# Rearranging the opening of a hybrid attention and RG-LRU block: a broadcast by DMA, scale matrices and casts on GpSimd, one extra product

## The chip, the cores and the metric

The kernel runs on one core of one Trainium2 chip. A core has five engines that run their own instruction streams and meet through semaphores: TensorE (PE, with its weight loads shown as PEld), VectorE (DVE), ScalarE (ACT), GpSimd (POOL) and SyncE (SP), which here only issues DMAs. The metric is the device time of one execution in microseconds.

## The reference, cut to what matters

One decoder layer with a final norm: x is 1024 x 1024 fp32 (sequence by model width), c is one row of 1024. Only the first lines matter for this change:

```python
mod = c @ w_ada[l] + b_ada[l]
shift, scale, gate = jnp.split(mod, 3, axis=-1)
h = rmsnorm(x, norm_g[l]) * (1.0 + scale[:, None, :]) + shift[:, None, :]
proj = h @ w_in[l]
q, k, v, g_attn, xr, g_rnn, m_attn, m_rnn = jnp.split(proj, SPLIT_POINTS, axis=-1)
```

Behind it come sliding-window attention with sinks and partial rotary embedding (angle = position times a frequency), a gated linear recurrence (RG-LRU) behind a short convolution, two projections, a merge by sigmoid gates, an output projection, the residual and a last RMSNorm.

## The kernel before

Every large product is made in three matmuls of half-precision-like parts: each operand is cast to a high part (fp32r) and the rest, and high x high, rest x high and high x rest are summed. The large input projection behind the opening goes over pairs of output columns with seven half-size products for eight, in an order that a small planner writes out; attention and the two projections follow. None of that is changed.

The change is in the opening (lines 184 to 489), which makes h, transposed, in eight row blocks of 128 of its 1024 columns (index `kc`), and multiplies the first four column chunks of `w_in` (`START`, chunks 0, 1, 34 and 35, called `c` 0 to 3 there) with it. Its engines run in exactly the order in which the code issues (`manual_schedule`, line 181), each engine its own instructions, so an instruction that waits holds up all that stands behind it on its engine. The steps:

- Loads. On SP: eight tiles of x (`xt`, 128 x 1024, 512 KB each), then `w_ss`, the transposed modulation weights (`load_ss(kc)`: two 512 KB tiles for a `kc`), and halves of the first weight chunks (`load_s`), in turns. On ACT's queue: c as two half rows, and `pk`, a 128 x 96 table of small parameters. On POOL's queue: positions (`posr`) and the rotary frequencies (`invf`).
- c on all partitions. Two fp32 products on PE (line 248) with a row of ones put c into PSUM for 128 partitions; DVE copies them to `c_bc` (lines 384 and 385).
- Norm and transposes, a loop over the eight tiles of x (lines 390 to 398). `square(i)` on ACT sums the squares; `mean(i)` on DVE; `root(i-1)` on ACT; `scaled(i-1)` on DVE takes the reciprocal and scales the tile, or, for the tiles in `DIAG` (0 and 2), makes a diagonal matrix `dg` instead (line 346), by which PE scales while it transposes; `flip(i-1)` on PE makes eight 128 x 128 transposes into PSUM (line 359, or line 361 as a matmul with `dg`). `out_of(j, p, engine)` copies transposed blocks to SBUF (`xT`), on ACT (line 367) or DVE (line 369); the table `late` says at which turn of the loop.
- Modulation. `modulate(kc)` on DVE (line 258): two products of `w_ss` tiles with `c_bc`, summed along the row. `scales_of(kc)` on ACT (lines 263 and 265) makes scale and shift of the 128 rows, with `bng` (line 381) as an offset. `hi_parts(kc)` on ACT (lines 375 and 378) makes the high part `hh` in two halves and the full value; `lo_parts(kc)` on DVE (line 421) the rest `hl`.
- Weights. `cast_s(c, i)` on ACT (line 100) makes the high part `wh` of a half chunk, `rest_s(c, i)` on DVE (line 106) the rest `wl`. `first(kc, terms, cs)` on PE (line 434) makes the products: "h" is wh x hh, "w" is wl x hh, "l" is wh x hl. The first of them, `first(0, "h", (2, 3, 0, 1))`, needs `hi_parts(0)` and the four casts; `first(1, "h")` needs `hi_parts(1)`; `first(0, "w")` needs the four rests.
- Rotary angles. `angles()` on POOL (lines 286 to 321): 36 small steps on 128 x 64 and 128 x 128 tiles, wanted by a sine on ACT in line 469. Before the change they are issued all at once, ahead of the loop, and nothing else of the opening is behind them on POOL.

The last of the opening's work on ACT, in order: four `out_of(2, p)`, casts of c 2 and 3, `out_of(3, 0)`, `scales_of(0)`, `hi_parts(0)`, cast of c 0, `out_of(3, 3)`, cast of c 1, `scales_of(1)`, `hi_parts(1)`.

Of the kernel before, what the change touches and what calls it, by code (L numbers as in the profile page):

```python
# [12 lines left out]
F32 = mybir.dt.float32  # L13
# [5 lines left out]
ALU = mybir.AluOpType  # L19
# [3 lines left out]
P = 128  # L23
S = 1024
D = 1024
KC = 8
HALF = 512
# [6 lines left out]
PK_C, PK_BSH, PK_BSC, PK_NG, PK_CW, PK_CB, PK_BA, PK_BX, PK_LAM = (  # L34
    0, 8, 16, 24, 32, 64, 72, 80, 88)
# [9 lines left out]

SL = [slice(0, HALF), slice(HALF, S)]
XT = 12
DIAG = 0, 2


@with_exitstack
def tile_hybrid_block(ctx, tc, x, pk, rows, posr, posi, invf, c_row, w_ss, w_gate, w_main, w_v,
                      w_g, w_ap, w_rp, w_out, out):
    nc = tc.nc
    V, A, G, T = nc.vector, nc.scalar, nc.gpsimd, nc.tensor

# [23 lines left out]
    pk_t = const.tile([P, PK_N], F32, name="pk_t")  # L80
    ident = const.tile([P, P], F32, name="ident")
# [16 lines left out]
    def cast(dst, src, scale=1.0):  # L98
        if scale == 1.0:
            A.copy(dst[0][:], src)  # L100
        else:
            A.activation(dst[0][:], src, AF.Copy, scale=scale)  # L102
# [81 lines left out]
    starts = [new_ps(), new_ps(), bk[2:], bk[:2]]  # L184
    N_ST = len(starts)
    START = (0, 1, 34, 35)
    with ExitStack() as st:
        sp = st.enter_context(tc.tile_pool(name="start", bufs=1, side="right"))
        c_row_t = [wp.tile([P, HALF], F32, tag="ws", name="c_row_t", bufs=3)[0:1, :]
                   for _ in range(2)]  # L190
        for i in range(2):
            dma(c_row_t[i], c_row[:, SL[i]], A)
        dma(pk_t[:], pk, A)
        posr_t = sp.tile([P, 64], I32, name="posr_t")
        dma(posr_t[:], posr, G)
        invf_t = sp.tile([P, 1], F32, name="invf_t")
# [3 lines left out]
        xt, wada = [], {}  # L200
        for i in range(8):
            t = sp.tile([P, D], F32, tag="xt", name="xt", bufs=XT)
            dma(t[:], x[i * P:(i + 1) * P, :])
            xt.append(t)

        def load_ss(kc):
            for a in (1, 0):
# [4 lines left out]
        sw = [[None, None] for _ in starts]  # L212
        raw = {}
# [1 line left out]
        def load_s(c, i):  # L215
            raw[c, i] = load_half(w_main[START[c]][:, SL[i]])

        def cast_s(c, i):
            sw[c][i] = slot()
            cast(sw[c][i], raw[c, i])  # L220

        def rest_s(c, i):
            rest(sw[c][i], raw[c, i])
# [13 lines left out]
            load_ss(kc)  # L237
        rv = [load_half(w_v[i // 2][:, SL[i % 2]]) for i in range(4)]

        one_row = sp.tile([1, P], F32, name="one_row")  # L240
        warm = sp.tile([P, 1], F32, name="warm")
        V.memset(warm[:], 1.0)
        V.memset(one_row[:], 1.0)
        A.activation(warm[:], warm[:], AF.Sqrt)
        c_bc = sp.tile([P, D], F32, name="c_bc")
        psc = starts[0]
        for hf in range(2):
            T.matmul(psc[hf], one_row[:], c_row_t[hf], start=True, stop=True)
# [22 lines left out]
        def rnd(name, src, unit, n=64):  # L271
            m = 1.5 * 2.0 ** 23 * unit
            t = tiny(name, n)
            G.tensor_scalar(out=t[:], in0=src, scalar1=m, scalar2=m, op0=ALU.add,
                            op1=ALU.subtract)
            return t

        def pair_of(name, a, b, op=ALU.subtract, n=64):
            t = tiny(name, n)
            G.tensor_tensor(out=t[:], in0=a, in1=b, op=op)  # L280
            return t
# [4 lines left out]
        def angles():  # L286
            posf, ang = tiny("posf"), tiny("ang")
            G.tensor_copy(posf[:], posr_t[:])
            G.tensor_scalar(out=ang[:], in0=posf[:], scalar1=invf_t[:, 0:1], scalar2=None,
                            op0=ALU.mult)  # L290
            units = (2.0 ** 20, 2.0 ** 9, 2.0 ** -3)
            cons = [_split_const(u) for u in units]
            sums, tmp = [tiny(n) for n in ("sa", "sb", "sc_")], tiny("tmp")
            left = ang
            for i, unit in enumerate(units):
                piece = rnd(f"t{i}", left[:], unit)
                left = pair_of(f"a{i}", left[:], piece[:])
                for which, t in enumerate(sums):
                    k = float(cons[i][which] / unit)
                    o = t if i == 0 else tmp  # L300
                    G.tensor_scalar(out=o[:], in0=piece[:], scalar1=k, scalar2=None,
                                    op0=ALU.mult)
                    if i:
                        G.tensor_tensor(out=t[:], in0=t[:], in1=tmp[:], op=ALU.add)
            sa, sb, sc_ = sums
            ra = rnd("ra", sa[:], 1.0)
            fa = pair_of("fa", sa[:], ra[:])
            tt = pair_of("tt", fa[:], sb[:], ALU.add)
            rt = rnd("rt", tt[:], 1.0)
            ft = pair_of("ft", tt[:], rt[:])  # L310
            G.tensor_scalar(out=tmp[:], in0=left[:], scalar1=1.0 / (2.0 * math.pi),
                            scalar2=None, op0=ALU.mult)
            G.tensor_tensor(out=sc_[:], in0=sc_[:], in1=tmp[:], op=ALU.add)
            G.tensor_tensor(out=trn[:, 1, :], in0=ft[:], in1=sc_[:], op=ALU.add)
            G.tensor_scalar(out=trn[:, 0, :], in0=trn[:, 1, :], scalar1=0.25, scalar2=None,
                            op0=ALU.add)
            r2 = rnd("r2", trf, 1.0, 128)
            G.tensor_tensor(out=trf, in0=trf, in1=r2[:], op=ALU.subtract)
            G.tensor_scalar(out=trf, in0=trf, scalar1=2.0 * math.pi, scalar2=3.1415925,
                            op0=ALU.mult, op1=ALU.min)  # L320
            G.tensor_scalar(out=trf, in0=trf, scalar1=-3.1415925, scalar2=None, op0=ALU.max)

        ss = tiny("ss", 8)
        rr = tiny("rr", 8)
# [13 lines left out]
        def scaled(i):  # L338
            r1 = rr[:, i:i + 1]
            V.reciprocal(r1, r1)  # L340
            if i not in DIAG:
                V.tensor_scalar(out=xt[i][:], in0=xt[i][:], scalar1=r1, scalar2=None,
                                op0=ALU.mult)
            else:
                dg[i] = sp.tile([P, P], F32, tag="dg", name="dg", bufs=2)
                V.tensor_scalar(out=dg[i][:], in0=ident[:], scalar1=r1, scalar2=None,
                                op0=ALU.mult)

        dg = {}
# [3 lines left out]
        def flip(i):  # L353
            for kc in range(KC):
                c0 = kc // 4 * 256 + i % 2 * P
                o = banks[i // 2 % 2][kc % 4][:, c0:c0 + P]
                x_ = xt[i][:, kc * P:(kc + 1) * P]
                if i not in DIAG:
                    T.transpose(o, x_, ident[:])
                else:  # L360
                    T.matmul(o, x_, dg[i][:], start=True, stop=True)

        def out_of(j, p, eng):
            src = banks[j % 2][p].rearrange("p (a t) -> p a t", a=2)
            dst = xall[p][:, :, j * 256:(j + 1) * 256]
            if eng is A:
                A.copy(dst, src)
            else:
                V.tensor_copy(dst, src)

        def hi_parts(kc):
# [41 lines left out]
        out_of(3, 3, A)  # L413
        cast_s(1, 0)
        modulate(1)
        csn = sp.tile([P, 3, 64], F32, name="csn")

# [1114 lines left out]
    late, high, loaded = [], [], {}  # L1532
# [285 lines left out]
```

## Time and profile before

| what | value |
|---|---|
| median of three runs | 941.1 us (939.51 to 945.45) |
| the profiled execution's own time | 942.38 us |
| its span, first to last instruction | 940.3 us |
| PE busy in the span | 916.8 us (98%) |
| DVE, ACT, POOL busy | 679.5, 543.2, 119.3 us |
| mean granted TensorE clock | 0.994 |
| DMA moved | 164.21 MB, mean 175 GB/s |

A row of the timeline gives the start in us from the start of the span, the length, the engine, the line, the operation, the tiles written and read (output first), the shapes, how many instructions are merged in the row, and in brackets how long the engine was idle before it and what ended that. A row of the stage view gives the stretch, its length, the busy time of PE, PEld, DVE, ACT and POOL in it, the granted clock, the DMA engines' busy share and GB/s. A row of the chain gives start, length and what. In a row of groups the figures behind the bar are total busy us and mean ns of one, then idle time before them. A row of DMA issues ends in the median us from issue to landing.

### The profile page before, as it was taken

The page shows a single profiled execution, that of the slowest core. Times are in us where ns is not written, and L with a number is a line of the kernel's source. Part 1 is how long each engine was busy: PE and PEld are TensorE (multiplying, and loading weights), DVE is VectorE, ACT ScalarE, POOL GpSimd, SP SyncE. Part 2 cuts the span into 40 slices and gives each one's busy share as a digit, 9 for nine tenths or more (in the row PEclk, how much of TensorE's full clock was granted, in tenths as well). Part 3 has the DMA queues.
Part 4 walks back from the last instruction along what each step waited for, and adds up shares of the span by engine and source line. Part 5 has one row for each costly group of instructions (what it writes and reads, how often), then busy time and mean ns, then how long its engine had stood idle before and what let it go on. Part 6 is the DMA issues. An engine that isn't in the chain of part 4 may idle for free.

```text
span 940.3 us, 12460 instructions
## 1 busy us (share of the span) xinstructions
PE 916.8 (98%) x4277; PEld 754.9 (80%) x4277; DVE 679.5 (72%) x1003; ACT 543.2 (58%) x1053; POOL 119.3 (13%) x218
## 2 busy tenths in 40 slices
PE   6899999999999999999999999999999999999997
PEld 5689877888888788888888887788888888888886
DVE  5998597777659955885786786798999737656522
ACT  6866545554567755966585874787887622212311
POOL 6320050000000000000000001354454300000000
PEclk9899999999999999999999999999999999999999
DMA  9815578471332532452334258897656186536311
GB/s 346 317 55 202 179 268 268 141 268 52 113 113 101 172 128 71 145 201 90 113 112 157 101 169 259 282 369 226 217 177 195 57 308 221 168 130 219 135 73 68
DMA packets 80919, 164.21 MB, mean 175 GB/s; under 512 B 12532, under 2 KB 28916, under 8 KB 80856
## 3 DMA queue, kind: packets, MB, share of 16 engines
q1 hardware_dynamic: 77732, 156.02, 48.6%
q0 software_dynamic: 2256, 6.03, 2.0%
q10 hardware_dynamic: 868, 1.36, 0.4%
q8 instruction: 34, 0.56, 0.3%
q14 instruction: 29, 0.24, 0.1%
HBM read 114.00 MB, written 49.78 MB: 174 GB/s over the span
## 4 chain that ended last, share of the span: by engine, by line
PE 72%; DVE 10%; DMA 10%; ACT 5%; issue 3%; SPq 0%; POOL 0%; ACTq 0%; DVEq 0%
PE bk L628 40%; PE rp L169 7%; PE pgate L937 5%; PE rp L1683 3%; PE pmain L1683 3%; DMA wo<-w_out 3%; PE pmain L434 2%; PE bk L434 2%; PE pv L1251 2%; PE s_ps L1178 2%; DMA smr<-smr_d 1%; DMA tt<-tr_d 1%; PE pt L1217 1%; DVE wl L106 1%; DMA r<-w_ap 1%
## 5 line engine op out<-in xcount | busy, mean ns | idle before, releaser
L628 PE MATMUL bk<-nh,wh 128*128 128x512 f32 x368 | 145.1, 394 | 0.0
L628 PE MATMUL bk<-nl,wh 128*128 128x512 f32 x368 | 144.4, 392 | 0.0
L628 PE MATMUL bk<-nh,wl 128*128 128x512 f32 x368 | 143.0, 389 | 0.0
L106 DVE TENSOR_TENSOR wl<-r,wh 128x512 fp32r<-128x512 f32 x109 | 79.2, 733 | 14.3 <-ACT wh L100 14.2
L100 ACT CAST wh<-r 128x512 fp32r<-128x512 f32 x109 | 67.0, 618 | 34.6 <-DMA r<-w_ap 11.8
L628 PEld LDWEIGHTS bk<-nl,wh 128*128 128x128 f32 x368 | 69.1, 188 | 15.9
L628 PEld LDWEIGHTS bk<-nh,wl 128*128 128x128 f32 x368 | 69.2, 188 | 15.5
L628 PEld LDWEIGHTS bk<-nh,wh 128*128 128x128 f32 x368 | 69.3, 188 | 14.6 <-ACT wh L102 0.9
L628 PE MATMUL bk<-hh,wh 128*128 128x512 f32 x184 | 72.4, 394 | 0.0
L628 PE MATMUL bk<-hl,wh 128*128 128x512 f32 x184 | 72.2, 392 | 0.0
L628 PE MATMUL bk<-hh,wl 128*128 128x512 f32 x184 | 71.5, 388 | 0.0
L106 DVE TENSOR_TENSOR wl<-ws,wh 128x512 fp32r<-128x512 f32 x76 | 51.5, 684 | 4.4 <-ACT wh L100 4.4
L1203 ACT ACTIVATE p<-p,small 128x129 f32<-128x129 f32 x128 | 50.1, 401 | 0.0
L100 ACT CAST wh<-ws 128x512 fp32r<-128x512 f32 x76 | 45.7, 615 | 3.2 <-DVE ws L650 1.5
L628 PEld LDWEIGHTS bk<-hl,wh 128*128 128x128 f32 x184 | 34.5, 188 | 8.0
L1178 PE MATMUL s_ps<-ks,qs 128*128 128x256 f32 (+1 forms) x256 | 38.6, 294 | 2.3 <-DMA qs<-q_d 2.2
L628 PEld LDWEIGHTS bk<-hh,wl 128*128 128x128 f32 x184 | 34.5, 188 | 7.7
L628 PEld LDWEIGHTS bk<-hh,wh 128*128 128x128 f32 x184 | 34.6, 188 | 6.9
L802 POOL MEMSET xr<- 128x3 f32 x8 | 0.8, 101 | 309.9 <-PE pgate L937 233.4
L628 PE MATMUL bk<-hha,wl 128*128 128x512 f32 x92 | 36.1, 392 | 2.1 <-DVE wl L106 1.5
L741 ACT ACTIVATE c<-bk 128x512 f32<-128x512 f32 x29 | 17.3, 597 | 34.3 <-PE bk L628 34.2
L1700 ACT ACTIVATE o<-xo 128x1024 f32<-128x1024 f32 (+2 forms) x10 | 8.9, 890 | 47.5 <-DVE xo L1699 47.5
(351 smaller groups left out, 2297.1 us busy)
## 6 DMA issues: line engine op xcount, KB each, us to landing
r<-w_main SPq DMA_DIRECT2D x100, 256.0 KB, 4.2
wada<-w_ss SPq DMA_DIRECT2D x16, 512.0 KB, 8.2
qs<-q_d SPq DMA_DIRECT2D x16, 512.0 KB, 5.4
ks<-k_d SPq DMA_DIRECT2D x24, 192.0 KB, 3.8
xt<-x SPq DMA_DIRECT2D x8, 512.0 KB, 8.0
sma_d<-c SPq DMA_DIRECT2D x16, 256.0 KB, 3.5
wg<-w_gate SPq DMA_DIRECT2D x8, 512.0 KB, 5.1
q_d<-rhi SPq DMA_DIRECT2D x16, 256.0 KB, 4.6
```

The source lines that it names most:

```text
L100: A.copy(dst[0][:], src)
L106: V.tensor_tensor(out=dst[1][:], in0=src, in1=f32(dst[0][:]), op=ALU.subtract)
L169: mm = T.matmul(ps[hf], ww, xx[kc][hf], start=(kc == 0 and ww is w_h and xx is xh), stop=(kc == KC - 1 and xx is xl))
L434: T.matmul(starts[c][hf], ww[:, c0:c0 + P], xh[kc][hf], start=(kc == 0 and t_ == "h"), stop=(kc == KC - 1 and t_ == "l"))
L628: W["pe"] = T.matmul(ps, ww[:, c], b[kc][xx_], start=(first and kc == 0 and i == 0), stop=(kc == 3 and i == 2), skip_group_check=not first)
L741: A.activation(t["t"], s(), AF.Tanh, scale=0.5)
L937: W["pe"] = T.matmul(ps[:, SL[hf]], ww[:, c0:c0 + P], xx_[:, SL[hf]], start=(ic == 0 and i == 0), stop=(ic == 1 and i == 2))
L1178: W["pe"] = T.matmul(o, qs[:, j, qc], ks[:, b, k0 + (0 if n else P):k0 + 256], start=(b == 0), stop=(b == 1))
L1203: A.activation(px[:, j, :], px[:, j, :], AF.Exp, bias=sm[:, 0, j:j + 1], accum_out=sm[:, 1, j:j + 1])
L1217: W["pe"] = T.transpose(pt[:, j, :], px[:, j, 0:P], ident[:])
L1251: W["pe"] = T.matmul(pv[:], b, m[:].rearrange("p j q -> p (j q)"), start=(i == 0), stop=(i == len(prods) - 1))
L1683: T.matmul(ps[:, sl], lhs[k][th][:, ts_], w[:, sl], start=(k == 0 and w is h_ and lhs is mh), stop=(k == KC - 1 and lhs is ml))
```

## The change

- c comes to all partitions by one DMA on SP (a row of DRAM read for 128 partitions, 512 KB written), behind the eight x tiles; the two half rows, the row of ones, the two products and the two copies are gone. `pk` is loaded on SP behind it instead of on ACT's queue.
- `DIAG` gets tile 4, so that tile is scaled by PE too; the diagonal matrices are made on POOL.
- `angles()` becomes a generator that yields behind each step. Three steps are issued ahead of the loop, four behind each `scaled(i-1)`, and the last five behind the casts.
- The copies `out_of` are dealt out anew between DVE and ACT; `bng` moves behind `modulate(0)` on DVE.
- The four first casts go to POOL, in one go behind the loop and ahead of the last angle steps.
- Behind the last transposes PE gets one fp32 product, the identity by half of x tile 6, into a bank that the next product overwrites.

```diff
-DIAG = 0, 2
+DIAG = 0, 2, 4
...
-        c_row_t = [wp.tile([P, HALF], F32, tag="ws", name="c_row_t", bufs=3)[0:1, :]
-                   for _ in range(2)]
-        for i in range(2):
-            dma(c_row_t[i], c_row[:, SL[i]], A)
-        dma(pk_t[:], pk, A)
...
+        c_bc = sp.tile([P, D], F32, name="c_bc")
+        dma(c_bc[:], c_row.to_broadcast([P, D]))
+        dma(pk_t[:], pk)
...
-        def cast_s(c, i):
+        def cast_s(c, i, eng=A):
             sw[c][i] = slot()
-            cast(sw[c][i], raw[c, i])
+            if eng is G:
+                G.tensor_copy(sw[c][i][0][:], raw[c, i])
+            else:
+                cast(sw[c][i], raw[c, i])
...
-        for hf in range(2):
-            T.matmul(psc[hf], one_row[:], c_row_t[hf], start=True, stop=True)
...
             G.tensor_copy(posf[:], posr_t[:])
+            yield 1
             G.tensor_scalar(out=ang[:], in0=posf[:], scalar1=invf_t[:, 0:1], scalar2=None,
                             op0=ALU.mult)
+            yield 1
...
-                V.tensor_scalar(out=dg[i][:], in0=ident[:], scalar1=r1, scalar2=None,
+                G.tensor_scalar(out=dg[i][:], in0=ident[:], scalar1=r1, scalar2=None,
                                 op0=ALU.mult)
...
-        angles()
-        late = {1: [lambda: V.scalar_tensor_tensor(
-                    out=bng[:], in0=pk_t[:, PK_BSC:PK_BSC + 8], scalar=1.0,
-                    in1=pk_t[:, PK_NG:PK_NG + 8], op0=ALU.add, op1=ALU.mult),
-                    lambda: V.tensor_copy(c_bc[:, SL[0]], psc[0])],
-                2: [lambda: V.tensor_copy(c_bc[:, SL[1]], psc[1])],
-                3: [lambda: out_of(0, 0, V), lambda: out_of(0, 1, V)],
-                4: [lambda: out_of(0, 2, V), lambda: out_of(0, 3, V)],
+        angle = angles()
+
+        def turn(n=100):
+            for _ in range(n):
+                if next(angle, 0) == 0:
+                    break
+
+        turn(3)
+        late = {3: [lambda: out_of(0, 0, V), lambda: out_of(0, 1, V)],
+                4: [lambda: out_of(0, 2, V), lambda: out_of(0, 3, A)],
                 5: [lambda: out_of(1, 0, V), lambda: out_of(1, 1, V)],
-                6: [lambda: out_of(1, 2, A), lambda: out_of(1, 3, A)]}
+                6: [lambda: out_of(1, 2, A), lambda: out_of(1, 3, V)]}
...
                 root(i - 1)
                 scaled(i - 1)
+                turn(4)
                 flip(i - 1)
...
         flip(7)
-        for c in (2, 3):
-            cast_s(c, 0)
+        for i in range(1):
+            T.matmul(bk[i], ident[:], xt[6][:, SL[i]], start=True, stop=True)
+        for c in (2, 3, 0, 1):
+            cast_s(c, 0, G)
+        turn()
         modulate(0)
-        out_of(3, 0, A)
+        V.scalar_tensor_tensor(out=bng[:], in0=pk_t[:, PK_BSC:PK_BSC + 8], scalar=1.0,
+                               in1=pk_t[:, PK_NG:PK_NG + 8], op0=ALU.add, op1=ALU.mult)
+        for p in range(3):
+            out_of(3, p, A)
         scales_of(0)
         hi_parts(0)
-        out_of(3, 1, V)
-        cast_s(0, 0)
-        out_of(3, 2, V)
-        out_of(3, 3, A)
-        cast_s(1, 0)
+        out_of(3, 3, V)
         modulate(1)
```

More of the change, by code (lines that the diff above doesn't have):

```diff
@@ L238, in tile_hybrid_block @@
         rv = [load_half(w_v[i // 2][:, SL[i % 2]]) for i in range(4)]
-        one_row = sp.tile([1, P], F32, name="one_row")
         warm = sp.tile([P, 1], F32, name="warm")
         V.memset(warm[:], 1.0)
-        V.memset(one_row[:], 1.0)
         A.activation(warm[:], warm[:], AF.Sqrt)
-        c_bc = sp.tile([P, D], F32, name="c_bc")
-        psc = starts[0]
-        for hf in range(2):
-            T.matmul(psc[hf], one_row[:], c_row_t[hf], start=True, stop=True)
         mods = sp.tile([P, 16], F32, name="mods")
@@ L296, in angles @@
                 piece = rnd(f"t{i}", left[:], unit)
+                yield 1
                 left = pair_of(f"a{i}", left[:], piece[:])
+                yield 1
                 for which, t in enumerate(sums):
@@ L302, in angles @@
                                     op0=ALU.mult)
+                    yield 1
                     if i:
                         G.tensor_tensor(out=t[:], in0=t[:], in1=tmp[:], op=ALU.add)
+                        yield 1
             sa, sb, sc_ = sums
             ra = rnd("ra", sa[:], 1.0)
+            yield 1
             fa = pair_of("fa", sa[:], ra[:])
+            yield 1
             tt = pair_of("tt", fa[:], sb[:], ALU.add)
+            yield 1
             rt = rnd("rt", tt[:], 1.0)
+            yield 1
             ft = pair_of("ft", tt[:], rt[:])
+            yield 1
             G.tensor_scalar(out=tmp[:], in0=left[:], scalar1=1.0 / (2.0 * math.pi),
                             scalar2=None, op0=ALU.mult)
+            yield 1
             G.tensor_tensor(out=sc_[:], in0=sc_[:], in1=tmp[:], op=ALU.add)
+            yield 1
             G.tensor_tensor(out=trn[:, 1, :], in0=ft[:], in1=sc_[:], op=ALU.add)
+            yield 1
             G.tensor_scalar(out=trn[:, 0, :], in0=trn[:, 1, :], scalar1=0.25, scalar2=None,
                             op0=ALU.add)
+            yield 1
             r2 = rnd("r2", trf, 1.0, 128)
+            yield 1
             G.tensor_tensor(out=trf, in0=trf, in1=r2[:], op=ALU.subtract)
+            yield 1
             G.tensor_scalar(out=trf, in0=trf, scalar1=2.0 * math.pi, scalar2=3.1415925,
                             op0=ALU.mult, op1=ALU.min)
+            yield 1
             G.tensor_scalar(out=trf, in0=trf, scalar1=-3.1415925, scalar2=None, op0=ALU.max)
+            yield 1
         ss = tiny("ss", 8)
```

## The prediction

> **What bounds the kernel now.** I read the page first, then the chain of work that ended last, then the busy time by stage, then the opening engine by engine.
>
> ```profile
> PE 916.8 (98%) x4277; PEld 754.9 (80%) x4277; DVE 679.5 (72%) x1003; ACT 543.2 (58%) x1053; POOL 119.3 (13%) x218
> ```
>
> TensorE (PE) is busy for 98% of the span, so the opening decides only when it starts to run without a gap. The chain, around that moment (start, length, what):
>
> ```profile
> 29.34 0.82 ACT hha L375
> 30.17 0.04 issue
> 30.21 2.35 PE pmain L434 x4
> 32.56 1.71 PE bk L434 x4
> ...
> 50.03 2.77 PE bk L434 x12
> ```
>
> From 30.21 on the chain stays on PE: the first products of row block 1 (`first(1, "h")`) waited for `hi_parts(1)` on ScalarE. Before that PE had done only the eight products of block 0. The rows also show a slow stretch: 12 products take 2.77 us (0.231 us each) at 50 us, but four take 1.71 us (0.43 each) at 32.56. The stage view says why (stretch, length, PE, PEld, DVE, ACT, POOL busy, granted clock, DMA share, GB/s):
>
> ```profile
> 17.50:20.92 3.42, 2.36 (x19) 2.06 (x20) 3.31 (x10) 2.14 (x6) 2.93 (x7) 1.00 1.04 399
> 24.33:27.74 3.41, 1.46 (x4) 0.67 (x4) 3.38 (x7) 3.34 (x5) 3.09 (x5) 0.95 1.03 397
> 30.21:34.57 4.36, 4.36 (x10) 3.22 (x11) 4.33 (x6) 2.29 (x3) 2.13 (x4) 0.54 1.04 392
> 594.35:597.77 3.42, 1.93 (x6) 0.81 (x6) 2.52 (x5) 3.33 (x12) 1.27 (x2) 0.95 1.06 356
> 597.77:601.18 3.41, 3.41 (x15) 3.16 (x15) 3.33 (x8) 2.18 (x5) 0.99 (x2) 0.55 0.52 175
> ```
>
> The granted clock is 0.54 from 30.21 to 34.57, right behind a stretch in which PE worked 1.46 of 3.41 us; at 597.77 it halves again behind 1.93 of 3.42; behind 2.36 of 3.42 it stays at 1.00. So there are two things to gain: an earlier 30.21, and the half clock behind it. What PE did until then:
>
> ```profile
> 2.35 3.97 PE L248 MATMUL pmain<-c_row_t,one_row 1*128 1x512 f32 x4 [2.35 <-DMA c_row_t<-c_row]
> 7.99 3.78 PE L361 MATMUL bk<-dg,xt 128*128 128x128 f32 x16 [1.67 <-DVE dg L346]
> 11.82 1.94 PE L359 MATMUL bk<-ident,xt 128*128 128x128 f32 x8
> 13.56 2.06 PE L361 MATMUL pmain<-dg,xt 128*128 128x128 f32 x16
> 20.59 1.96 PE L359 MATMUL pmain<-ident,xt 128*128 128x128 f32 x16
> 25.40 0.50 PE L434 MATMUL bk<-hha,wh 128*128 128x512 f32 x1 [2.85 <-ACT hha L375]
> ```
>
> Block 0 is transposed by 16 half-speed matmuls (3.78 us; the same work takes 2.06 later), block 1 in 1.94. The last transposes end at 22.55.
>
> **The change, part by part.**
>
> (1) Block 0's scale matrix `dg[0]` moves to GpSimd (POOL), which works strictly in the order written, behind `turn(3)`: the first three steps of the rope angles.
>
> ```profile
> 9.73 0.46 POOL L289 TENSOR_SCALAR ang<-posf,invf_t 128x64 f32<-128x64 f32 x1 [3.06 <-DMA invf_t<-invf]
> 10.81 0.32 POOL L280 TENSOR_TENSOR a<-ang,t 128x64 f32<-128x64 f32 x1
> 14.43 0.37 POOL L301 TENSOR_SCALAR tmp<-t 128x64 f32<-128x64 f32 x1
> 18.60 0.37 POOL L301 TENSOR_SCALAR tmp<-t 128x64 f32<-128x64 f32 x1
> 21.63 1.32 POOL L274 TENSOR_SCALAR ra<-sa 128x64 f32<-128x64 f32 x1
> 28.02 0.65 POOL L314 TENSOR_TENSOR trn<-ft,sc__303 128x64 f32<-128x64 f32 x1
> 32.06 0.53 POOL L321 TENSOR_SCALAR trn<-trn 128x128 f32<-128x128 f32 x1
> ```
>
> The second of these steps waits until 9.73 for `invf_t`, a load that the change leaves where it is; the fourth starts at 10.81. So `dg[0]` starts near 10.8. A 128x128 operation with a scalar took 0.53 on POOL (0.29 on VectorE, below): `dg[0]` is ready at 11.35 instead of 7.94, and PE starts 3.4 us later. Blocks 0 and 1 then take the slow 5.8 us (7.99 to 13.76) and end near 17.2. Bounds: 14.5, if the clock opens at once (2.06 for block 0 and, as the last 16 transposes took 1.96, 1.0 for block 1), and 13.8, if `invf` lands as early as needed.
>
> (2) `dg[2]` stands eight angle steps further (10.81 to 14.43, so 3.6 us): ready at 15.5, while PE is busy until 17.2, so it is free. `dg[4]` stands eight more steps on (14.43 to 18.60, 4.2 us): ready at 20.2. PE does block 2 to 19.3, block 3 to 20.4 and block 4 to 22.5, so it is just in time; block 4 now costs 2.06 there instead of about 1.
>
> ```profile
> 7.65 0.29 DVE L346 TENSOR_SCALAR dg<-ident,rr 128x128 f32<-128x128 f32 x1
> 14.62 0.75 DVE L342 TENSOR_SCALAR xt<-xt,rr 128x1024 f32<-128x1024 f32 x1
> 17.40 1.28 DVE L369 COPY xT<-pmain 128x512 f32<-128x512 f32 x2
> 25.27 1.22 DVE L258 SCALAR_TENSOR_TENSOR jk<-wada,c_bc 128x1024 bf16<-128x1024 f32 x1
> 27.68 2.87 DVE L106 TENSOR_TENSOR wl<-r,wh 128x512 fp32r<-128x512 f32 x4
> ```
>
> VectorE (DVE) loses two scale matrices (0.6), two `c_bc` copies (same shape as the copies at 17.40, 0.64 each) and block 4's scaling (0.75): 2.6 us. But it now waits for PE's late blocks. After block 3 (20.4) it has two copies (1.28), block 5's scaling (0.9 with its reciprocal), a copy (0.64), blocks 6 and 7 (0.9 each): done at 25.0. The last transposes then end near 26.5, 4 us after 22.55.
>
> (3) The tail on ScalarE (ACT) loses four casts and gains one copy.
>
> ```profile
> 20.46 2.06 ACT L367 COPY xT<-bk 128x512 f32<-128x512 f32 x4 [0.56 <-PE bk L359]
> 22.38 1.17 ACT L100 CAST wh<-r 128x512 fp32r<-128x512 f32 x2
> 23.89 0.43 ACT L263 ACTIVATE gsc<-mods,bng,pk_t 128x1 f32<-128x1 f32 x1
> 24.53 0.81 ACT L375 ACTIVATE hha<-xT,shf,gsc 128x512 fp32r<-128x512 f32 x1
> 25.25 0.80 ACT L375 ACTIVATE hhb<-xT,shf,gsc 128x512 fp32r<-128x512 f32 x1
> ```
>
> Copies and casts pass at 0.515 each (2.06 for four). Three copies behind the late transposes and 0.64 of scales (23.89 to 24.53) put `hi_parts(0)` at 28.3 (24.53 before) and PE's first product at 29.2. From block 0's `hha` to block 1's ACT needs 4.81 us now (24.53 to 29.34), of which two casts and a copy are 1.55; so block 1's `hha` starts at 31.5 and PE goes on at 32.35 instead of 30.21: **+2.1 us**. The `modulate` products of DVE (four at 1.25 from 25.0, a copy between) end at 30.9, in time.
>
> (4) POOL must have the four casts done by then. Twelve angle steps come first. They took 18.60 to 28.67 before, because DVE's two-input products stretched them: 1.32 for `ra` where the step at 18.60, of the same shape, took 0.37. Now DVE starts those products at 25.0, so most steps run at their short times: 12 of about 0.45 from 20.2 end near 26; the other end is 30.3. Nothing shows a cast of this shape on POOL. The nearest rows:
>
> ```profile
> 58.30 0.66 POOL L532 CAST mgt<-mf 128x128 uint32<-128x128 f32 x1
> L1237 POOL TENSOR_SCALAR_AFFINE_SELECT phm<-phc 128x512 fp32r<-128x512 f32 x28 | 18.5, 661 | 34.4 <-ACT phc L1222 34.4
> ```
>
> I take 0.66, the row with the same shape and types; the high end is the other row by size, 2.6. While DVE runs its 1.25 us products one POOL operation gets in per product, so the four end at 26 + 4 x 1.25 = 31 and cost nothing: PE needs the last at 31.9. The four `wl` rests on DVE (2.87) follow to 33.8; PE needs the third of them at 34.2. [...]
>
> (5) The one fp32 product in the gap (`ident` by half of `xt[6]`): two instructions, half of the 3.97 us of L248's four at the slow clock, so 1 to 2 us, from 26.5 to at most 28.5, before 29.2. It is free, and fills half of the gap ahead of the products. With the eight products' 1.9 us PE works more evenly, so I take the clock as open from 32.35. The eight products of block 1 then need 0.72 (the wait for `hhb`, 24.53 to 25.25) and 7 x 0.231, 2.3 us, instead of 4.06: **-1.7 us**. If it closes, nothing is given back.
>
> (6) The queues. `c_bc` adds 512 KB to SP's queue behind x.
>
> ```profile
> wada<-w_ss SPq DMA_DIRECT2D x2, 512.0 KB, 11.5
> 38.24 0.69 DVE L421 TENSOR_TENSOR hla<-xT,hha 128x512 fp32r<-128x512 f32 x1
> 43.86 0.40 PE L434 MATMUL pmain<-hla,wh 128*128 128x512 f32 x1
> ```
>
> The DMA engines are full (399 GB/s in the stretch from 17.50), so everything behind it comes 1.3 us later; twice that, if a row read 128 times comes at half rate. The first row is the first `wada` pair: issued from 6.03, it lands at about 17.5 and is now wanted at 25.0: hidden. ACT's three issues and L248 leave ACT and PE idle time; both wait for x anyway. DVE is some 4 us later from 31 on. Its `lo` part of block 2 began at 38.24, its second half ended 1.3 later, and PE read it at 43.86: a lead of 4.3, which is just eaten up. I count nothing for it, and up to 2 us in the range.
>
> Sum: +2.1 - 1.7 = +0.4 us. The profiled execution took 942.4 us (span 940.3), so 942.8; the median of the runs, 941.1, lies 1.3 below it, so I say 941.5.
>
> **The rivals.** *It works as meant*: the flips aren't late, because `invf` lands early or the clock opens at block 0 (14.5 instead of 17.2). The tail then moves 2.7 us forward, PE goes on at 29.7, and the clock holds: -0.5 - 1.7 = -2.2, with DVE's lighter load at most -4: 937 to 939. For it: ACT's 1.55 us. Against: the wait until 9.73, which stands ahead of `dg[0]`.
> *The product doesn't keep the clock*: PE does about 2.2 us of work between 28 and 32.35, near the share (1.46 of 3.41) behind which the clock halved. Then the -1.7 is lost: +2.1 to +3.8, 943 to 945. [...]
> *POOL becomes the bound* (slower): beyond 1.5 us a cast (26 + 4 x 1.5 = 32) PE waits for POOL. At 2.6 the last ends at 36.4, the rests 36.4 to 38 come behind it: +5 to +8, 946 to 949. Over 1% (9.4 us) needs 3 us a cast.
>
> **How the numbers follow.** Forecast 0.45 (940 to 943), as meant 0.25, clock lost 0.2, POOL 0.08, something else 0.02. The range 937 to 947 leaves out most of POOL's case and the ends of the others, under 0.15. A measurement here can tell about 1%, 9.4 us, from no change: faster 0.02, same 0.94, slower 0.04.
>
> **What would show it.** POOL's `dg` starting at 10.8 behind `ang`; the first matmul of L361 near 11.4; last transposes near 26.5; first product of block 1 near 32.3 at 0.23 us a product; four POOL casts of 0.66 to 1.3 between 26 and 31. The forecast is wrong if `ang` starts before 8, if a cast takes over 1.5, or if PE has a gap between 34 and 60, where DVE's lateness would show.

## The result, and the profile after

| | before | after |
|---|---|---|
| median, runs on the same chip | 943.7 us (939.51 to 951.6, 20 runs) | 946.7 us (944.15 to 951.0, 20 runs) |
| ratio after / before | | 1.0031, 95% interval 1.0016 to 1.0046 |
| profiled execution (span) | 942.38 us (940.3) | 946.52 us (944.8) |
| PE, DVE, ACT, POOL busy in the span | 916.8, 679.5, 543.2, 119.3 us | 912.7, 676.8, 541.5, 124.5 us |

The change costs 0.31%, some 2.9 us. That is inside the 1% called "same" above, but the interval excludes no change and excludes a gain. Most of it, 1.9 us, arises in the first 36 us; the rest comes later, and not in one place. To compare kernels I use one instant, called the **mark** from here on: the start of the first product with the low half of a weight (`first(0, "w")`). Sixteen products of the opening lie ahead of it in every kernel here, and from it up to 80 us PE waits for nothing, before or after.

Timeline of before, then of after, PE's row at the mark:

```profile
34.07 0.48 PE L434 MATMUL pmain<-hha,wl 128*128 128x512 f32 x1
```

```profile
35.95 0.40 PE L452 MATMUL pmain<-hha,wl 128*128 128x512 f32 x1
```

So the mark is 1.9 us late. The chain of waits of after, in order of time (start, length, what):

```profile
2.04 6.53 DMA invf_t<-invf
8.76 0.47 POOL ang L284
...
9.85 1.03 POOL dg L359
...
14.03 0.60 POOL dg L359
...
18.42 0.61 POOL dg L359
...
21.29 0.92 POOL ra L268
22.28 0.88 POOL fa L274
23.23 1.19 POOL tt L274
24.49 1.30 POOL rt L268
...
28.90 0.32 POOL trn L321
29.22 0.57 POOL wh L219
29.83 2.08 PE bk L452 x4
```

Before, the chain ahead of the products ended on ACT (`hha` of block 1). Now it runs on POOL alone, from the landing of `invf` to the first cast. POOL, busy 13% of the span, waits for no other engine from 8.76 to 32.4, and in its one row stand scale matrices, angle steps and casts. What the other engines did meanwhile, by the timeline:

```profile
10.93 3.68 PE L374 MATMUL bk<-dg,xt 128*128 128x128 f32 x16 [10.93 <-POOL dg L359]
14.45 1.04 PE L372 MATMUL bk<-ident,xt 128*128 128x128 f32 x8
...
22.16 1.97 PE L372 MATMUL pmain<-ident,xt 128*128 128x128 f32 x16 [0.16 <-DVE xt L355]
23.97 1.02 PE L421 MATMUL bk<-xt,ident 128*128 128x512 f32 x2
29.83 0.80 PE L452 MATMUL bk<-hha,wh 128*128 128x512 f32 x1 [4.83 <-POOL wh L219]
...
22.89 1.34 DVE L252 SCALAR_TENSOR_TENSOR jk<-wada,c_bc 128x1024 bf16<-128x1024 f32 x1
...
29.81 3.74 DVE L106 TENSOR_TENSOR wl<-r,wh 128x512 fp32r<-128x512 f32 x4 [1.16 <-POOL wh L219]
...
26.25 0.81 ACT L388 ACTIVATE hha<-xT,shf,gsc 128x512 fp32r<-128x512 f32 x1
...
29.54 0.81 ACT L388 ACTIVATE hha<-xT,shf,gsc 128x512 fp32r<-128x512 f32 x1
```

ACT had `hha` of block 0 at 27.06 (26.25 and 0.81). Of the 4.83 us that PE idled, the last 2.8 were thus for a cast on POOL alone; DVE waited 1.16 us for it. The stages, to be held against those shown of before:

```profile
17.50:20.92 3.42, 2.90 (x24) 2.67 (x25) 3.15 (x9) 2.66 (x7) 2.94 (x8) 1.00 1.05 394
24.63:28.04 3.41, 0.36 (x1) 0.00 (x0) 3.38 (x7) 3.21 (x7) 3.18 (x4) 1.00 1.04 402
28.18:35.00 6.82, 5.17 (x12) 3.86 (x13) 5.66 (x8) 4.09 (x6) 6.40 (x10) 0.51 0.94 326
597.77:601.18 3.41, 2.11 (x11) 1.34 (x11) 3.12 (x6) 3.07 (x12) 1.27 (x2) 1.00 1.06 339
```

PE worked 0.36 of 3.41 us, and then the granted clock was 0.51 from 28.18 to 35.00, as in before's opening (0.50 from 27.42 to 34.25). From the mark on I matched PE's instructions of the two traces in order. After is 1.8 to 2.2 us behind up to 130 us. At 136 PE waits longer for a `wl` of DVE than it did before (before, then after), which makes 3.0; why DVE is later there stays open.

```profile
135.42 0.51 PE L628 MATMUL bk<-hha,wl 128*128 128x512 f32 x1 [1.31 <-DVE wl L106]
138.44 0.51 PE L646 MATMUL bk<-hha,wl 128*128 128x512 f32 x1 [2.12 <-DVE wl L106]
```

At 570 us the lag is 3.3. At 600 it is 1.5, as the half clock that before shows there is missing (last row of the stages), but at 620 it is 2.8 again. It ends at 4.4 in these two executions; by the ratio the change costs 2.9.

### The profile page after: what moved, and what is told of

The parts are those of the page before. It is cut to its first block, busy times and chain, and to the rows that moved or that the text cites. A ratio compares the mean times of both kernels' runs of the same rounds, so it can differ in the third digit from the quotient of the medians.

```text
span 944.8 us, 12472 instructions
## 1 busy us (share of the span) xinstructions
PE 912.7 (97%) x4283; PEld 752.6 (80%) x4283; DVE 676.8 (72%) x996; ACT 541.5 (57%) x1050; POOL 124.5 (13%) x225
## 4 chain that ended last, share of the span: by engine, by line
PE 72%; DMA 12%; DVE 8%; ACT 3%; issue 2%; POOL 2%; SPq 0%; DVEq 0%; ACTq 0%; POOLq 0%
PE bk L646 39%; PE rp L169 8%; PE pgate L955 5%; PE rp L1701 3%; PE pmain L1701 3%; DMA wo<-w_out 3%; PE pmain L452 3%; PE bk L452 2%; PE s_ps L1196 2%; PE pv L1269 2%; DMA tt<-tr_d 1%; DMA r<-w_rp 1%; DMA yl<-yl_d 1%; PE pt L1235 1%; PE pmain L169 1%
## 5 line engine op out<-in xcount | busy, mean ns | idle before, releaser
L100 ACT CAST wh<-r 128x512 fp32r<-128x512 f32 x105 | 64.5, 618 | 34.0 <-DMA r<-w_ap 10.5
L646 PEld LDWEIGHTS bk<-hh,wl 128*128 128x128 f32 x184 | 34.5, 188 | 7.7
L646 PE MATMUL bk<-hha,wh 128*128 128x512 f32 x92 | 36.1, 393 | 0.0
```

The source lines that it names most:

```text
L646: W["pe"] = T.matmul(ps, ww[:, c], b[kc][xx_], start=(first and kc == 0 and i == 0), stop=(kc == 3 and i == 2), skip_group_check=not first)
```

## The experiments

All ratios are to the kernel before, run beside the experiment on the same chip. The chip's runs spread, so each interval is about 2 us to either side. The marks come from one profile each, and some of their differences are chance: in `no_product` and `five_products` the casts on POOL start 0.6 us earlier than in after (28.53 and 28.57 against 29.16), though nothing ahead of them on POOL was changed; `dg[0]`, behind the same three steps, took 1.03 in after and 0.62 in `angles_first`.

| run | first product | mark | ratio, 95% interval |
|---|---|---|---|
| before | 25.40 | 34.07 | 1 |
| after | 29.83 | 35.95 | 1.0031 (1.0016 to 1.0046) |
| angles_last | 26.37 | 32.46 | 1.0096 (1.007 to 1.0121) |
| angles_first | 33.30 | 38.72 | 1.0066 (1.0044 to 1.0088) |
| dg_dve | 27.61 | 33.45 | 1.0005 (0.9984 to 1.0026) |
| casts_act | 27.50 | 35.25 | 1.0041 (1.0017 to 1.0064) |
| five_products | 29.24 | 34.27 | 1.0025 (1.0 to 1.005) |
| no_product | 29.19 | 35.34 | 1.0049 (1.0029 to 1.0069) |
| dma_alone | 24.06 | 32.04 | 0.9994 (0.9973 to 1.0014) |
| dma_products | 24.35 | 31.60 | 0.9994 (0.9974 to 1.0015) |
| middle3 | 25.80 | 31.60 | 0.9978 (0.9958 to 0.9999) |
| middle_bng | 24.85 | 30.49 | 0.9982 (0.9961 to 1.0002) |

The theory after the result: POOL's row, with the angle steps ahead of the casts in it, sets PE's start, and the gap that it opens halves the clock. The rivals: ACT's tail is the bound anyway; the casts are too slow on POOL; the later transposes cost it.

**The dose of angle steps.** `angles_last` issues all 36 steps behind the casts, `angles_first` all of them ahead.

```diff
-        turn(3)
...
-                turn(4)
```

> The mark in all runs is the start of the first product of first(0, "w"), behind sixteen others: 34.07 us before, 35.95 us with the change. Here all 36 angle steps stand behind the four casts on POOL; dg[0], dg[2], dg[4] and the casts have nothing ahead of them there. Theory P (POOL's order: the casts wait behind 31 angle steps, and the 4.8 us gap they make also halves the clock): dg[0] near 7.7 instead of 9.85, casts done by 25 instead of 32.4, first product near 25 instead of 29.83, mark at 30.5 with an open clock and 32.2 with a halved one; the time 3.5 to 5 us under that of the change, 1.5 to 3.5 under before. Rival C (only the clock: PE has a gap whatever POOL does, and the halved clock costs the 1.7 us): first product may come earlier, but the mark stays within 1 us of 35.95. Rival F (late transposes, from dg on POOL and PE scaling a third tile): mark 34.5 to 35, time within 1.5 us of the change.

The mark came at 32.46, 3.5 earlier than with the change, where both rivals had it at 34.5 or later, and yet the run is the slowest of all. Its timeline (POOL's casts, PE, DVE, then ACT):

```profile
21.05 4.27 POOL L219 CAST wh<-r 128x512 fp32r<-128x512 f32 x4 [4.07 <-DMA r<-w_main]
...
26.37 0.47 PE L450 MATMUL bk<-hha,wh 128*128 128x512 f32 x1 [3.19 <-ACT hha L388]
...
21.07 1.66 DVE L252 SCALAR_TENSOR_TENSOR jk<-wada,c_bc 128x1024 bf16<-128x1024 f32 x1
...
55.44 0.31 ACT L485 ACTIVATE csn<-trn 128x128 f32<-128x128 f32 x1 [9.12 <-POOL trn L333]
...
59.60 1.22 PE L450 MATMUL pmain<-hh,wh 128*128 128x512 f32 x2 [7.12 <-ACT wh L100]
```

The casts are now done when ACT is (25.3), so ACT sets the first product. But the 36 steps beside DVE's products and `lo` parts run from 25.26 to 55.40, 0.84 us each, and ACT, in order, waits 9.12 us at its sine; the casts behind the sine come late, PE idles 7.12 us, and the granted clock is 0.50 from 55.2 to 65.4. The theory on the start holds; for the total it fell, as it counted nothing for the sine, which ACT reached at 46.3.

For the other end:

```diff
-        for c in (2, 3, 0, 1):
-            cast_s(c, 0, G)
         turn()
+        for c in (2, 3, 0, 1):
+            cast_s(c, 0, G)
```

> The dose the other way: the last five angle steps, which took 0.69, 0.83, 0.47, 0.97 and 1.02 us, stand ahead of the casts too (all 36 of them). Theory P: casts begin 3.5 to 4.3 us later, near 33, first product near 33.6, mark 38.5 to 39.5, time 2.5 to 3.5 us above that of the change. Rivals C and F: the steps are hidden, mark within 0.5 us of 35.95, no change in time.

```profile
32.63 3.20 POOL L219 CAST wh<-r 128x512 fp32r<-128x512 f32 x4
...
33.30 0.79 PE L452 MATMUL bk<-hha,wh 128*128 128x512 f32 x1 [7.57 <-POOL wh L219]
```

Five more steps ahead of the casts move these by 3.47 us (29.16 to 32.63), the first product by 3.47 and the mark by 2.8. The start follows POOL's row one to one.

**The scale matrices.** `dg_dve` puts them back on DVE.

```diff
-                G.tensor_scalar(out=dg[i][:], in0=ident[:], scalar1=r1, scalar2=None,
+                V.tensor_scalar(out=dg[i][:], in0=ident[:], scalar1=r1, scalar2=None,
```

> The changed kernel with the three scale matrices back on VectorE (blocks 0, 2 and 4 all stay scale matrices); everything else as changed. In the changed kernel GpSimd is never idle from 8.76 to 32.4, and its three scale matrices take 1.03, 0.61 and 0.60 of that. Theory (GpSimd's one row of work sets PE's start, so each step in it counts at full length): the casts start about 2.2 us earlier, at 26.8 to 27.3, the first product comes at 27.4 to 28.2 instead of 29.8, and the mark at 33.5 to 34.6 instead of 35.95. Rival, by the prediction's step 1 (the scale matrices count through the late transposes): the flips start 1 to 2 us earlier and the last transposes end before 23.5, but the casts start after 28.5 and the mark stays at 35.5 or later. Total by the theory 944.5 to 946, by the rival 946.5.

Timeline of this run:

```profile
26.95 3.21 POOL L219 CAST wh<-r 128x512 fp32r<-128x512 f32 x4
...
21.19 1.02 PE L421 MATMUL bk<-xt,ident 128*128 128x512 f32 x2
27.61 0.80 PE L452 MATMUL bk<-hha,wh 128*128 128x512 f32 x1 [5.40 <-POOL wh L219]
```

The three matrices took 2.24 us of POOL's row; the casts came 2.21 earlier and the mark 2.5 (33.45, just ahead of the expected span), with the total back at before's. The transposes came 2.8 earlier too (the product behind them at 21.19 instead of 23.97), but that gave PE only a longer wait for POOL, 5.40. The matrices cost through POOL's row, not through the transposes.

**The casts.** `casts_act` puts the casts back on ACT, where before has them.

```diff
-        for c in (2, 3, 0, 1):
-            cast_s(c, 0, G)
         turn()
+        for c in (2, 3):
+            cast_s(c, 0)
...
         out_of(3, 3, V)
+        cast_s(0, 0)
+        cast_s(1, 0)
```

> The changed kernel with its four casts back on ScalarE where the kernel before has them: blocks 2 and 3 ahead of ScalarE's last evictions, blocks 0 and 1 behind block 0's hha; all remaining angle steps stay on GpSimd. Theory (the casts behind the angle steps set PE's start): the first product no longer waits for GpSimd and comes right behind hha of block 0, which two casts of 0.66 put from 26.25 to about 27.5; PE then waits for the casts of blocks 0 and 1 (about 30 to 31) and for block 1's hha at about 32; the mark at 34.3 to 35.9, near that of the kernel before (34.07), and VectorE's modulates keep about 1.23 instead of up to 1.7. Rival (ScalarE's own chain is the bound whichever engine casts): the mark at 36 or later. Total 943 to 946 beside 946.7 for the changed kernel.

```profile
27.50 0.50 PE L454 MATMUL bk<-hha,wh 128*128 128x512 f32 x1 [2.63 <-ACT hha L388]
30.97 0.82 ACT L388 ACTIVATE hha<-xT,shf,gsc 128x512 fp32r<-128x512 f32 x1
```

The first product came at 27.50, behind `hha`, the mark at 35.25: inside the theory's span, but only 0.7 better than with the change, and the time (1.0041) isn't better at all. With the casts, ACT's row becomes the bound: its `hha` of block 1 moves from 29.54 to 30.97. So taking the casts off ACT was no mistake; what stood ahead of them on POOL was.

**The clock.** `five_products` issues five fp32 products instead of one, `no_product` none.

```diff
-        for i in range(1):
-            T.matmul(bk[i], ident[:], xt[6][:, SL[i]], start=True, stop=True)
+        for i in range(5):
+            T.matmul(bk[0], ident[:], xt[6][:, SL[0]], start=True, stop=True)
```

> Five of the fp32 products instead of one behind the last transposes: 24.0 to about 29, so that the 4.8 us gap on PE is filled and the first product at 29.83 comes at the same time or up to 0.3 later. Theory P says the casts still set the first product (29.8 to 30.1), and only the halved clock behind it can go: mark 34.0 to 34.3, time 1.5 to 2 us under that of the change, level with before. Rival C expects the same gain here, but then none from moving the angle steps. If the one product already did all that such products can do, mark 35.95 to 36.3 and no change in time.

```profile
23.65 4.46 PE L421 MATMUL bk<-xt,ident 128*128 128x512 f32 x10
29.24 0.50 PE L452 MATMUL bk<-hha,wh 128*128 128x512 f32 x1 [1.13 <-POOL wh L219]
...
23.00:30.00 7.00, 5.87 (x21) 2.87 (x20) 6.06 (x11) 6.90 (x14) 6.60 (x9) 1.00 1.03 404
```

The first rows are of the timeline, the last of the stage view: a gap of 1.13, the clock 1.00, and the mark at 34.27, 1.7 ahead of the change. The first product came 0.6 earlier with the casts, by chance, so the open clock was worth 1.1 us of that: from the first product to the mark PE needed 5.03 us instead of 6.12. The total is not clear of the change's (1.0025 against 1.0031). In this profile the lead is lost at 136 us, where the clock halves behind a wait (stage view):

```profile
133.45:136.86 3.41, 1.41 (x7) 0.82 (x6) 3.38 (x6) 2.08 (x5) 3.06 (x5) 1.00 1.11 356
136.86:140.27 3.41, 3.41 (x8) 2.74 (x9) 3.41 (x6) 1.74 (x3) 1.00 (x2) 0.50 0.49 193
```

> The changed kernel without its one fp32 product behind the last flip. Its product ended at 25.0 and the gap behind it was 4.8 us, the clock half from 28.2 to 35.0. Theory (the product does nothing while the gap behind it is longer than about 3 us): the first product is at 29.8 as before, the clock halves one stretch earlier or at the same time, and the mark stays at 35.95 less or more 0.3; if the half stretch starts 3.4 us earlier and ends 3.4 us earlier, at 31.6, the mark comes about 1.0 to 1.5 earlier, at 34.5 to 35. Rival (the product is worth something even so): the mark at 36.5 or later.

The mark came 0.6 earlier, between the two spans that I had set. The first product came 0.6 earlier too, with the casts. The clock halved at 27.45 instead of 28.04, and ended its slow stretch 0.6 earlier. So no effect of the one product shows: with a gap of 4.83 us (after) or 5.42 (`no_product`) ahead of the first product, the clock halved either way.

**The loads alone.** `dma_alone` is before with the broadcast of c by DMA, `pk` behind x and `bng` behind `modulate(0)`; all else stays. `dma_products` adds two fp32 products behind `flip(7)`.

> The kernel before with one part of the change alone: c broadcast by DMA behind x and the small table behind it, the two fp32 products, two DVE copies and three issues on ACT gone; bng behind modulate(0). With the change the third tile of x landed 1.3 us earlier (8.08 against 9.34). Theory P: this part is no loss: blocks 1 to 7 pass 0.7 to 2 us earlier, mark 32.1 to 33.4 with the clock halved as before, time 0.7 to 2 us under before. Rival (the 512 KB more on a full DMA queue cost): the modulation weights arrive late and the mark is 34.5 to 36.

```profile
24.06 0.57 PE L423 MATMUL bk<-hha,wh 128*128 128x512 f32 x1 [2.90 <-ACT hha L367]
...
24.40:31.20 6.80, 6.43 (x13) 3.46 (x13) 6.76 (x11) 6.30 (x10) 6.23 (x8) 0.50 1.03 401
```

The opening moves forward: the last sixteen transposes start at 19.20 instead of 20.59, and the mark comes 2.0 us earlier. How much of this is of the loads stays open: ACT could start on the third x tile at 9.42 in before and at 8.16 in after, but DVE came to that tile's `mean` at 9.35 in after and at 9.82 in `angles_last`, with the same loads. Behind the gap of 2.90 the clock was half all the same (0.50 from 24.40 to 31.20, last row, of the stage view). The time can't be told from before's; the 0.7 to 2 us that I expected there don't show.

> The kernel before with the c broadcast by DMA, pk behind x and bng behind modulate(0), as in the run with the loads alone, and in addition two fp32 products into bk[0] behind the last flip; the scale matrices and the casts stay where they were. The mark (start of the first product of block 0's low weight halves, 16 products into the chunks) stood at 32.04 with the loads alone, where the clock was half from 24.4 to 31.2. If the price of the half clock is 16 products' difference (0.43 less 0.23 each, less what the wait for block 1's hha at 28.0 takes away), the two products of about 1 us close the gap from 21.1 to 24.1 to less than 1 us, the clock stays open, and the mark comes at 30.2 to 30.6, 1.4 to 1.8 earlier. Rival: block 1's hha at 28.0 and the casts behind it hold PE anyway, and the mark stays at 31.5 to 32.0. The total, if the mark's gain is kept: 937 to 940 beside a before of 942.5; if it is eaten later: 940 to 942.

The clock stayed open (stage view of this run):

```profile
24.40:31.20 6.80, 4.70 (x15) 2.51 (x16) 6.76 (x11) 6.59 (x10) 6.23 (x8) 1.00 1.04 404
```

Yet the mark gained 0.4 us, not 1.4 to 1.8: PE waits for casts, `hha` and `hhb` on ACT between the products: these waits add up to 2.10 us here (0.21, 0.82, 0.26, 0.60 and 0.21), where the timeline of `dma_alone` shows none. That is the rival that I had written down. From the first product to the mark the open clock was worth 0.7 us here (7.25 instead of 7.98), and 1.1 in `five_products`, where the waits add up to 0.58.

**Due times.** `middle3` deals the steps out by when their results are wanted: none stands ahead of the first scale matrix, 6, 9 and 8 behind the three of them, the casts follow, and the last 13 come behind these, as only the sine wants them; three products hold the clock.

```diff
-        turn(3)
...
-                turn(4)
+                turn({1: 6, 3: 9, 5: 8}.get(i, 0))
...
-        for i in range(1):
-            T.matmul(bk[i], ident[:], xt[6][:, SL[i]], start=True, stop=True)
+        for i in range(3):
+            T.matmul(bk[0], ident[:], xt[6][:, SL[i % 2]], start=True, stop=True)
```

> The changed kernel with its 36 angle steps laid out otherwise: none ahead of the scale matrices, 6, 9 and 8 behind the three of them, the last 13 behind the casts; three fp32 products in place of one. Theory (the steps between the last scale matrix and the casts set PE's start, and the steps behind the casts cost only if the Sin waits for them): dg[0] at 7.7 and dg[4] at 16 to 17, the casts start when the weights are there at about 21 and end by 25.5, the first product follows hha at 26.2 to 26.6 with the clock open, the mark is at 30.5 to 31.5 (32.5 if the clock halves), and the 13 steps left end near 38 to 40, ahead of the Sin's turn at about 46, so that no wait for trn shows and the gain of 4.5 to 5.5 us over the changed kernel at the mark is kept to 130 us: total 939 to 943. Rival (the 13 steps beside VectorE's modulates and lo parts slow these enough to take the gain back): the mark as above, but the lead over the changed kernel shrinks below 2 us by 80 us, total 944 to 947.

```profile
22.57 4.27 POOL L219 CAST wh<-r 128x512 fp32r<-128x512 f32 x4
...
25.80 0.47 PE L451 MATMUL bk<-hha,wh 128*128 128x512 f32 x1 [0.79 <-ACT hha L388]
...
29.15 0.50 PE L451 MATMUL pmain<-hha,wh 128*128 128x512 f32 x1 [0.86 <-ACT hha L388]
```

The last step ends at 39.0, well ahead of the sine. The mark is 4.35 us ahead of the change's (31.60, 0.1 past the span that I had set), and 4.0 of that are left at 130 us. The ratio, 0.9978, is the lowest here. Against the change that is clear; against before it is the only one whose interval lies below 1, and only just, which is weak among eleven. The casts end 1.3 us later and the first product comes 0.6 us earlier than I expected.

`middle_bng` mends DVE's order on top: `bng` up into the loop, block 3's last eviction behind `modulate(1)`.

```diff
-                6: [lambda: out_of(1, 2, A), lambda: out_of(1, 3, V)]}
+                6: [lambda: out_of(1, 2, A), lambda: out_of(1, 3, V),
+                    lambda: V.scalar_tensor_tensor(
+                    out=bng[:], in0=pk_t[:, PK_BSC:PK_BSC + 8], scalar=1.0,
+                    in1=pk_t[:, PK_NG:PK_NG + 8], op0=ALU.add, op1=ALU.mult)]}
...
-        out_of(3, 3, V)
         modulate(1)
+        out_of(3, 3, V)
```

> The kernel of the middle3 run (casts on GpSimd ahead of the angle steps that can wait, three fp32 products) with VectorE's order mended: bng goes up into the loop over the blocks, and block 3's last eviction goes behind modulate(1). In middle3 VectorE spent 0.56 on bng and 0.68 on that eviction between the two modulates, hha of block 1 came at 28.29 behind the second of them, and PE waited 0.86 for it; ScalarE had waited 0.42 for bng. Theory (modulate(1) on VectorE is now the bound of PE's second start): hha of block 1 starts at 27.0 to 27.4, the first product at 25.4 or so, PE's pause before block 1 is 0.3 us or less, and the mark is at 30.3 to 30.7 instead of 31.60: total 939.5 to 941, ratio to before 0.996 to 0.998. Rival (ScalarE's own row or the casts hold it): the mark stays at 31.3 to 31.7 and the total at 941.3.

```profile
22.15 5.27 POOL L219 CAST wh<-r 128x512 fp32r<-128x512 f32 x4
...
26.91 0.50 PE L452 MATMUL pmain<-hha,wh 128*128 128x512 f32 x1 [0.49 <-POOL wh L219]
28.05 0.51 PE L452 MATMUL pmain<-hha,wh 128*128 128x512 f32 x1
```

The wait for `hha` ahead of block 1 (at 28.05) is gone and the mark is at 30.49, as expected. PE now waits 0.49 us for a cast on POOL instead. The ratio (0.9982) isn't lower than `middle3`'s, with intervals too wide for 1.1 us.

**Marks and times.** A straight line through all kernels of the table but `angles_last` gives 1.07 us of time for 1 us of mark; the farthest kernel lies 1.6 us off, inside the intervals. `angles_last` lies some 9 us above the line, which is its late sine and the half clock behind it. So the opening is where these kernels differ, and over all of them the mark carries to the end about one to one. Single executions win or lose 1 to 4 us later on: `middle_bng` leads before by 3.6 us at the mark and by 2.3 at 135 us, and `five_products` loses its lead at 136 us. What decides these stays open.

## Why the prediction was right, and where it was wrong

The range (937 to 947) and the class "same" held. The point (941.5, or +0.4 by the sum) didn't: +2.9 by the ratio, +1.9 at the mark. Of the 5.2 us between 941.5 and 946.7, 2.6 are not the change's: the point stood on the median of three runs, 941.1, and over twenty before's is 943.7. That the range held is in part luck, since 946.7 lies 0.3 us inside its end, and in the 946 to 949 of "POOL becomes the bound", which had a chance of 0.08 and is, by another way, what happened. None of the three signs that I had set for a wrong forecast showed (`ang` at 8.76, casts under 1.5 us, no PE gap from 34 to 60): none of them watched when the casts start. Point by point:

- Step 1, `dg[0]` at 10.8: came at 9.85. `invf` landed at 8.57 and `ang` started at 8.76 instead of 9.73. That is of the loads, as in `dma_alone`, where nothing else moves, `ang` starts at 8.55; I had named the case and given it to a rival. The matrix took 1.03, not 0.53, beside DVE's scaling; the two later ones took 0.60 and 0.61. PE was at full speed from block 1 on, which took only 1.04.
- Step 2: the last transposes ended at 24.1 instead of 26.5. Right in kind (late), 2.4 too large.
- Step 3: block 1's `hha` at 29.54, not 31.5. ACT's lighter row did what it should, and ACT was no longer the bound.
- **Step 4 failed**: "most steps run at their short times: 12 of about 0.45 from 20.2 end near 26". They ran from 19.10 to 29.22, the "other end" that I had written beside it. As the transposes were early, DVE's two-input products began at 22.89 instead of 25.0, right across these steps: `ra` 0.91, `fa` 0.87, `tt` 1.18, `rt` 1.29. The two estimates hung together, and I took the good end of both. The casts themselves were no trouble. They took 0.61 us while DVE waited for them and 1.07 beside its `wl`. Beside `modulate`, where step 4 had them at 1.25, three of the four took about 1.60 in `middle_bng`. My rival "POOL becomes the bound" asked for 1.5 us a cast, and POOL became the bound at a mean of 0.80, because the casts started 3 us later than I had put them. `angles_first`, `angles_last` and `dg_dve` show it: the start follows POOL's row.
- **Step 5 failed** behind it: one product of 1.02 us did not hold the clock across a gap of 4.83. The rival "the product doesn't keep the clock" came about, by another way than its own. The price that I gave it, 1.7 us, was too high: the mark of `five_products` comes 1.7 earlier, but 0.6 of that is its earlier first product, and the clock is worth 1.1.
- Step 6, queues and DVE's lead: no PE gap between the mark and 60 us, as said.

With the clock held, `five_products` stands 0.2 us behind before at the mark, where my sum had 0.4; that is near by chance, as an earlier tail and a later POOL cancel in it, and as the casts came 0.6 us earlier by chance.

## What to carry to other kernels

Work moved to an engine that is 13% busy was not free here, as that engine's row, in order, was not empty when the work became due (five more steps ahead of the casts moved the first product by 3.47 us): add up what stands ahead of it, at the durations that the steps have beside the neighbour engine (`ra` took 0.91 us in after and 1.32 in before, where a step of its shape took 0.37), and sort the row by due times. Moving everything behind the urgent work shifts the wait to the next due time (the sine: 9 us), so both ends have to be written down. The filler products held the clock where they left a gap of 0.26 to 1.20 us, and one product that left 4.83 did not; they gave 1.1 us where the products behind them waited 0.58 us for their inputs, and 0.7 where these waited 2.10.

## What the runs showed of the hardware

- GpSimd and VectorE were slower beside each other, in both directions. A cast of 128x512 on GpSimd took 0.61 us in after where DVE stood waiting for it, 1.07 beside DVE's `wl`, and about 1.60 beside `modulate` in `middle_bng`, three of its four; in before the four steps beside the first four products of `modulate` took 1.06 to 1.32, one step to a product; in after a `wl` took 0.72 with no cast beside it and 1.07 to 1.09 with one; the product of `modulate` took 1.22 to 1.34 beside the small steps of after and 1.50 to 1.66 where a cast had started first (`angles_last`, `middle3`). The rows are of after, then `middle_bng` (shortest, median and longest of the four casts in ns).

```profile
L219 POOL CAST wh<-r x4: 611/840/1076, 29.2 to 31.3; 128x512 fp32r<-128x512 f32 x4
L219 POOL CAST wh<-r x4: 612/1600/1608, 22.1 to 26.8; 128x512 fp32r<-128x512 f32 x4
```

- In the opening the clock halved after gaps of 2.63 (`casts_act`), 2.85 (before), 2.90 (`dma_alone`) and up to 7.57 us, and not after 0.26 to 1.20 us (`middle_bng`, `middle3`, `five_products`, `dma_products`). The half stretch lasted 6.83 us in before (27.42 to 34.25) and in after (28.04 to 34.87), but in `angles_last`, behind a gap of 3.19, the products start 0.43 us or more apart only from 28.12 to 31.30.
- The length of the gap alone didn't decide. At 136 us PE stood idle for 2.00 us in `five_products` and the clock halved, and for 2.12 in after and it stayed open. Up to 930 us, the changes of the granted clock lie whole multiples of 3.41 us apart in before (27.42, 34.25, 597.45, 600.86) and in after (28.04, 34.87), so these traces can be cut into windows on that grid. In `five_products` the idle time lay in the one window shown above, with PE busy for 1.41 of 3.41 us, and the clock was 0.50 in the next. In after it was spread over two, which were busy for 2.46 and 2.24 us:

```profile
133.86:137.27 3.41, 2.46 (x11) 1.69 (x9) 3.38 (x6) 1.35 (x4) 3.07 (x5) 1.00 1.08 381
137.27:140.68 3.41, 2.24 (x10) 1.84 (x11) 3.41 (x6) 2.20 (x4) 2.06 (x5) 1.00 0.83 315
```

- Cut so, the clock halves three times up to 930 us in before and after, from the start of the clock's record (13.77 and 14.39 us) on: behind windows in which PE was busy for 1.46 and 1.93 of 3.41 us (before, from 24.01 and from 594.03) and 0.36 (after, from 24.63). It stays open behind 1.94 (before, from 20.60) and 1.70 (after, from 574.17). So the busy time of one window doesn't decide either, and the exact rule stays open.
- Short half-clock stretches also come far from any change, and not in every kernel: from 577.20 to 583.60 `no_product` runs at 0.50 and after at 1.00. There 19 of PE's matmuls took 6.40 us, where after's 34 took 5.92; at after's 0.174 each the 19 come to 3.3, so the stretch cost some 3.1 us (an estimate from these two rows), about as much as the change itself, so a cause is read from the opening's rows and a time from the interval.
